# The last MLP-2 group of a hybrid trunk layer: another order of tiles, and another split of the finishing work between engines

## The chip, the cores and the metric

The kernel runs on one core of a Trainium2 chip. The metric is the device time of one execution in microseconds (us). All times below are us from the start of the profiled execution's span unless they say otherwise. TensorE (PE) multiplies, VectorE (DVE) and ScalarE (ACT) work element by element, POOL is GpSimd, and SP issues DMAs in the order in which the program gives them.

## The reference, cut to what matters

One trunk layer is computed for 1024 latent tokens and 128 context tokens. Only its last part bears on the change: the second product of the MLP, its RMS norm, and the gated sum.

```python
f = jnp.square(jax.nn.relu(jnp.einsum('btd,df->btf', h, lp['w_mlp1'])))
f = jnp.einsum('btf,fd->btd', f, lp['w_mlp2'])
x = x + gate2 * rms_norm(f, lp['g_post_mlp'])
```

`gate2` is one row of 1024 for latent tokens and another for context tokens, and the width of f is 4096. The outputs that the change touches are `y_sample` (tiles 0 to 7 of 128 tokens) and `y_prompt` (tile 8).

## The kernel before, in words

The nine token tiles keep an accumulator each in SBUF, `acc_t[i]`, 128 tokens x 1024. The 4096 rows of the second weight are worked off in eight groups (`mlp2(g, hooks)`, L2378, called from L2530). In a group, tile 8 comes first: two halves of 512 columns, 12 products each, into banks `s` and `P` (L2380 to L2389). Then come four rounds u over the pairs of tiles in `QUAD` (L2247), (0, 3), (1, 4), (2, 5), (6, 7), each of seven steps s by a Strassen-like scheme (`STEP2`, L2248): a step (u, s) has six products of 128x512, three on each half `e` of the round's activations. The text calls them round u and step (u, s). Steps of one round that share a letter in `STEP2` (x, y, z) accumulate in the same PSUM bank, and after every step `take` (L2340, L2344) has VectorE add the bank to an accumulator: x is steps 0, 2, 4, 6, z is steps 3 and 5. TensorE can go on in a bank only when it has been taken. Step 5 of a round completes its second tile, step 6 its first.

The activations of a round, `fT`, are two loads of 0.92 MB each (L2326) into one of two sets of buffers. `group_hooks` (L2414) puts the loads of round u + 2 behind step (u, 6) of round u, since they need its buffers: rounds 2 and 3 of a group are loaded behind (0, 6) and (1, 6), rounds 0 and 1 of the next behind (2, 6) and (3, 6). Every DMA here is issued by SP, in program order, and SP waits for whatever the next one needs.

In the last group, functions in `hooks` and two tables place the rest of the work by step. `Gate` (L1721) prepares the gate rows in `fz`: two GRd loads of 0.52 MB, and per quarter of 256 columns a bias row and a norm row (0.13 MB each, L1733, L1734), which VectorE adds and multiplies (`make`, L1740, L1741). Two quarters are made at (0, 4) and (0, 5), which then load the other two into the same two buffers (`mw`), made at (1, 2) and (1, 3). `x1_load(n)` (L2353) loads the residual of tile `FIN[n]`, 0.52 MB, into one of seven buffers `xs`: n = 0 to 6 at the steps (0, 0) to (0, 6), the last two when `finish_b` has freed a buffer. `finish_a(i)` (L2346) has ScalarE square the tile with a sum (L2348) and take the root (L2349); `finish_b(i)` (L2357) has VectorE take the reciprocal (L2359) and do a scaled multiply with the gate in two halves (L2364), and POOL add the residual (L2366; VectorE for the last tile), then SP stores the tile. `FIN` (L2351) is the order of finishing, `FA` and `FH` (L2411, L2412) the steps behind which each half stands. Tiles 7 and 6 are finished after the last step.

Every engine runs its own instructions in order: a gate operation that waits on VectorE holds the takes behind it.

## Time and profile before

| what | us |
|---|---|
| median of 3 runs | 1718.33 |
| lowest and highest of them | 1717.26, 1722.8 |
| the profiled execution's own time | 1720.11 |
| its span | 1718.3 |
| last group, first product | 1656.48 |
| last product of the kernel | ends at 1706.14 |
| busy in the span: PE, DVE, ACT, POOL | 1591.1, 1107.6, 803.4, 518.5 |

The span is the time between the first and the last recorded event of one execution; 1.8 us of that execution's time lie around it. A row of the timeline gives start, length, engine (PEld is TensorE's weight load, SPq is SP's DMA queue), line, operation, output and inputs by the program's names, shape and count; in brackets stands how long the engine was idle before and what released it. Consecutive instructions of one kind are merged into one row. The ends of products are modelled.

### The profile page before, as it was taken

The page shows a single profiled execution, that of the slowest core. Times are in us where ns is not written, and L with a number is a line of the kernel's source. Part 1 is how long each engine was busy: PE and PEld are TensorE (multiplying, and loading weights), DVE is VectorE, ACT ScalarE, POOL GpSimd, SP SyncE. Part 2 cuts the span into 40 slices and gives each one's busy share as a digit, 9 for nine tenths or more (in the row PEclk, how much of TensorE's full clock was granted, in tenths as well). Part 3 has the DMA queues.
Part 4 walks back from the last instruction along what each step waited for, and adds up shares of the span by engine and source line. Part 5 has one row for each costly group of instructions (what it writes and reads, how often), then busy time and mean ns, then how long its engine had stood idle before and what let it go on. Part 6 is the DMA issues. An engine that isn't in the chain of part 4 may idle for free.

```text
span 1718.3 us, 33433 instructions
## 1 busy us (share of the span) xinstructions
PE 1591.1 (93%) x13035; PEld 1341.4 (78%) x13035; DVE 1107.6 (64%) x1884; ACT 803.4 (47%) x1549; POOL 518.5 (30%) x593
## 2 busy tenths in 40 slices
PE   6799989889899999779998999999998899999996
PEld 2678777778788776657686999999998678888884
DVE  2734776586876887947648976777767334444457
ACT  3634443343425567626345666666676422222111
POOL 3100186767310220112120000000000487666635
PEclk9899989999999999989999999999999999999999
DMA  9544856674753768899843568777778755566667
GB/s 312 190 135 125 208 139 173 167 197 116 184 140 93 173 138 196 194 232 246 233 172 112 153 196 243 224 229 221 217 226 276 259 199 215 220 231 233 231 241 256
DMA packets 436030, 341.22 MB, mean 199 GB/s; under 512 B 106392, under 2 KB 396384, under 8 KB 435872
## 3 DMA queue, kind: packets, MB, share of 16 engines
q1 hardware_dynamic: 433760, 331.53, 66.0%
q0 software_dynamic: 2112, 7.55, 1.4%
q8 instruction: 102, 1.67, 0.4%
q14 instruction: 56, 0.46, 0.1%
HBM read 214.72 MB, written 124.29 MB: 197 GB/s over the span
## 4 chain that ended last, share of the span: by engine, by line
PE 68%; DVE 13%; DMA 7%; POOL 4%; ACT 4%; issue 3%; SPq 1%; DVEq 0%; POOLq 0%; ACTq 0%
PE ps_g L2399 9%; PE ps_g L2222 6%; PE ps_P L2222 6%; PE ps_G L2399 4%; PE ps_g L531 4%; PE ps_g L532 3%; PE ps_g L533 3%; PE ps_G L2222 3%; PE ps_g L1662 3%; PE ps_m L2399 2%; PE ps_m L1534 2%; PE ps_G L1503 2%; PE ps_m L2222 2%; DMA wm<-in_w_mod_dram 2%; PE ps_G L1519 2%
## 5 line engine op out<-in xcount | busy, mean ns | idle before, releaser
L531 PE MATMUL ps_g<-hH,wH 128*128 128x384 f32 x552 | 208.3, 377 | 2.6 <-DVE hH L270 1.9
L532 PE MATMUL ps_g<-hL,wH 128*128 128x384 f32 x552 | 190.8, 346 | 6.5 <-DVE hL L484 6.1
L533 PE MATMUL ps_g<-hH,wL 128*128 128x384 f32 x552 | 189.2, 343 | 0.0
L2312 POOL TENSOR_TENSOR sL<-w2r,sL 128x512 fp32r<-128x512 f32 x8 | 10.4, 1302 | 451.6 <-ACT sL L2311 451.6
L2344 DVE TENSOR_TENSOR acc<-ps_g,acc 128x512 f32<-128x512 f32 x116 | 80.0, 691 | 94.0 <-PE ps_g L2399 80.1
L531 PEld LDWEIGHTS ps_g<-hH,wH 128*128 128x128 f32 x552 | 107.0, 194 | 18.0 <-issue 8.4
L2222 PE MATMUL ps_P<-h2H,ws 128*128 128x384 f32 x432 | 118.3, 334 | 0.0
L532 PEld LDWEIGHTS ps_g<-hL,wH 128*128 128x128 f32 x552 | 107.3, 194 | 11.2 <-DVE hL L484 10.0
L2399 PE MATMUL ps_g<-sH,fT 128*128 128x512 f32 x408 | 109.9, 401 | 1.1 <-DVE acc L2344 1.1
L533 PEld LDWEIGHTS ps_g<-hH,wL 128*128 128x128 f32 x552 | 106.8, 194 | 0.0
L2399 PEld LDWEIGHTS ps_g<-sH,fT 128*128 128x128 f32 x408 | 77.7, 191 | 21.0 <-DVE acc L2344 2.4
L1024 POOL TENSOR_TENSOR ar<-ar 128x252 f32<-128x252 f32 (+22 forms) x124 | 80.8, 652 | 42.2 <-DMA ar<-NAd 33.4
L2120 ACT ACTIVATE ft<-ft 128x384 f32<-128x384 f32 x138 | 72.3, 524 | 42.4 <-DVE ft L2119 39.4
L1028 POOL TENSOR_TENSOR ar<-ar 128x252 f32<-128x252 f32 (+22 forms) x124 | 86.5, 697 | 9.2
L2222 PEld LDWEIGHTS ps_P<-h2H,ws 128*128 128x128 f32 x432 | 78.7, 188 | 0.0
L2399 PE MATMUL ps_G<-sL,fT 128*128 128x512 f32 x252 | 70.3, 401 | 5.2 <-ACT acc L2342 5.0
L2222 PE MATMUL ps_P<-h2L,ws 128*128 128x384 f32 x216 | 72.2, 334 | 0.0
L1539 DVE TENSOR_TENSOR SV<-ps_m,Dt 64x256 f32<-64x256 f32 x136 | 57.1, 421 | 23.3 <-PE ps_m L1534 17.0
L2344 DVE TENSOR_TENSOR acc<-ps_G,acc 128x512 f32<-128x512 f32 x60 | 41.4, 690 | 38.4 <-PE ps_G L2399 38.4
L2222 PE MATMUL ps_G<-oT,ws 128*128 128x384 f32 x336 | 63.9, 338 | 0.2 <-DVE ft L2119 0.2
L2311 ACT ACTIVATE sL<-tt 128x512 fp32r<-128x512 f32 x31 | 19.6, 632 | 94.1 <-POOL tt L2305 62.6
L2222 PE MATMUL ps_g<-oT,ws 128*128 128x384 f32 x336 | 63.0, 336 | 0.0
(522 smaller groups left out, 4177.0 us busy)
## 6 DMA issues: line engine op xcount, KB each, us to landing
Fd<-fs SPq DMA_DIRECT2D x224, 256.0 KB
fT<-Fd SPq DMA_DIRECT2D x64, 896.0 KB
KGd<-ar SPq DMA_DIRECT2D x96, 192.0 KB
r<-KGd SPq DMA_DIRECT2D x36, 512.0 KB
mw<-in_w_mod_dram SPq DMA_DIRECT2D x64, 256.0 KB
w1r<-in_w_mlp_dram SPq DMA_DIRECT2D x32, 512.0 KB
w2r<-in_w_mlp_dram SPq DMA_DIRECT2D x31, 512.0 KB
raw<-in_w_in_dram SPq DMA_DIRECT2D x26, 512.0 KB
```

The lines of the kernel that those rows point to most:

```text
L531: T.matmul(ps, wH[:, k, :], hH[b][:, k, :], start=(k == 0), stop=False)
L532: T.matmul(ps, wH[:, k, :], hL[b][:, k, :], start=False, stop=False)
L533: T.matmul(ps, wL[:, k, :], hH[b][:, k, :], start=False, stop=(k == 7))
L1024: E.tensor_tensor(out=t, in0=X[:, :, 0:m, j:j + 1].to_broadcast([128, 2, m, w]), in1=n[:, :, j % 8:j % 8 + 1, j + 1:32].to_broadcast([128, ...
L1028: E.tensor_tensor(out=X[:, :, 0:m, j + 1:32], in0=X[:, :, 0:m, j + 1:32], in1=t, op=ALU.subtract)
L1503: T.matmul(RU[n][r0:r0 + 32, 0, p, :], KRG[n][kq][:, e, p, kc, 0:32], SV[n][s % NSV][:, e, p, :], start=True, stop=True)
L1539: Q.add("V", cv(256), lambda e=e, ks=ks: V.tensor_tensor(out=SV[n][(s + 1) % NSV][ks, e], in0=x["S"][ks], in1=dv[ks], op=ALU.mult), r=[("S ...
L1662: T.matmul(z["ps"], y["t"][:, q // 2, k], wo_t[4 + k][q % 2][:, hs_], start=first, stop=last and stop)
L2120: S_ = lambda: [S.activation(out=f, in_=x, func=fn) for x, fn in ((src if add is None else f, AF.Relu), (f, AF.Square))]
L2222: T.matmul(ps[ch], w[:, qw, k], h[q][:, k, :], start=(new and k == n == 0), stop=(k == 3 and n == 2), skip_group_check=True)
L2344: V.tensor_tensor(out=acc_(i, h), in0=ps, in1=acc_(i, h), op=ALU.add)
L2399: T.matmul(ps[ch], f[:, OPI[fx], qf], w[:, qw], start=(new and e == n == 0), stop=(e == 1 and n == 2), skip_group_check=True)
```

## The change

In the last group, tile 8 comes after the four rounds (`unit_c`), and `FIN` puts it last. All four quarters of the gate's rows are loaded ahead of the first step, into two buffers (`r2`, `r3`) that the weights have left, and the eight gate operations stand one per step from (0, 2) to (1, 2). The residual loads 0 to 4 stand at (0, 1) to (0, 5), loads 5 and 6, into `r2` and `r3`, at (1, 5) and (1, 6). Tiles 3 and 0 (`FINP`) are finished at (1, 2): ScalarE scales them by the reciprocal, POOL multiplies with the gate and adds the residual, in halves. The other seven tiles are finished by VectorE alone, as four operations (multiply, add, multiply, add) that go into a list `dq`; from step (2, 4) on `pop` lets one out behind every step, three ahead of each take of tile 8, and the rest at the end. `finish_a` works on tile 8 in halves, as each is complete. Results are written into the accumulator rather than into the residual's buffer, and every output is stored in halves of 0.26 MB.

```diff
--- before.py
+++ after.py
@@ -1733,12 +1733,13 @@
             SY.dma_start(out=t[:, 0], in_=a["b_mod"][0, j * D + 256 * h:j * D + 256 * h + 256].partition_broadcast(128))
             SY.dma_start(out=t[:, 1], in_=a[self.gp][0, hs_].partition_broadcast(128))
 
-        def make(self, h):
+        def make(self, h, q=None):
             hs_ = slice(256 * h, 256 * h + 256)
             bb, gb = [self.t[h][:, q:q + 1].to_broadcast([128, 2, 256]) for q in range(2)]
             r = self.rows[:, :, hs_]
-            V.tensor_tensor(out=r, in0=r, in1=bb, op=ALU.add)
-            V.tensor_tensor(out=r, in0=r, in1=gb, op=ALU.mult)
+            for n, (x, op) in enumerate(((bb, ALU.add), (gb, ALU.mult))):
+                if q in (None, n):
+                    V.tensor_tensor(out=r, in0=r, in1=x, op=op)
 
     def gtmp(h):
         return wp.tile([128, 4, 128], F32, tag="mw", name="mw", bufs=2).rearrange("q (a b) d -> q a (b d)", a=2)
@@ -2343,40 +2344,65 @@
         else:
             V.tensor_tensor(out=acc_(i, h), in0=ps, in1=acc_(i, h), op=ALU.add)
 
-    def finish_a(i):
-        ss = fin_ss[i] = mp["ac"].tile([128, 1], F32, tag="ss", name="ss", bufs=4)
-        S.activation(out=wp.tile([128, D], F32, tag="raw", name="jk", bufs=1), in_=acc_t[i], func=AF.Square, accum_out=ss)
-        S.activation(out=ss, in_=ss, func=AF.Sqrt, scale=1.0 / D, bias=eps[:, 0:1])
-
-    FIN = (8, 3, 0, 4, 1, 5, 2, 7, 6)
+    FIN = (3, 0, 4, 1, 5, 2, 7, 6, 8)
+
+    FINP = (3, 0)
+    dq = []
+
+    def finish_a(i, h=None):
+
+        c = slice(0, D) if h is None else slice(512 * h, 512 * h + 512)
+        ss = mp["ac"].tile([128, 1], F32, tag="ss", name="ss", bufs=6)
+        S.activation(out=wp.tile([128, D], F32, tag="raw", name="jk", bufs=1)[:, c], in_=acc_t[i][:, c], func=AF.Square, accum_out=ss)
+        if h == 1:
+            V.tensor_tensor(out=ss, in0=ss, in1=fin_ss[i], op=ALU.add)
+        fin_ss[i] = ss
+        if h != 0:
+            S.activation(out=ss, in_=ss, func=AF.Sqrt, scale=1.0 / D, bias=eps[:, 0:1])
+            finish_b(i)
 
     def x1_load(n):
         x1_t[FIN[n]] = xs[n % 7]
         SY.dma_start(out=xs[n % 7], in_=X1d[FIN[n]][:])
 
     def finish_b(i):
-        ss, xt, t = fin_ss[i], x1_t[i], acc_t[i]
-        V.reciprocal(out=ss, in_=ss)
+        ss, t = fin_ss[i], acc_t[i]
+        gt, m = gt2["t"][:, 0 if i < 8 else 1], FIN.index(i)
         dst = o["sample"][0, 128 * i:128 * i + 128] if i < 8 else o["prompt"][0]
-        end = FIN.index(i) > 6
+        if i in FINP:
+            V.reciprocal(out=ss, in_=ss)
+            S.activation(out=t, in_=t, func=AF.Copy, scale=ss)
         for h in range(2):
             hs_ = slice(512 * h, 512 * h + 512)
-            V.scalar_tensor_tensor(out=t[:, hs_], in0=t[:, hs_], scalar=ss, in1=gt2["t"][:, 0 if i < 8 else 1, hs_], op0=ALU.mult,
-                                   op1=ALU.mult)
-            (V if i == FIN[-1] else G).tensor_tensor(out=xt[:, hs_], in0=t[:, hs_], in1=xt[:, hs_], op=ALU.add)
-            if end:
-                SY.dma_start(out=dst[:, hs_], in_=xt[:, hs_])
-        if not end:
-            SY.dma_start(out=dst, in_=xt)
-        if FIN.index(i) + 7 < NTILE:
-            x1_load(FIN.index(i) + 7)
+            if i in FINP:
+                G.tensor_tensor(out=t[:, hs_], in0=t[:, hs_], in1=gt[:, hs_], op=ALU.mult)
+                G.tensor_tensor(out=t[:, hs_], in0=t[:, hs_], in1=x1_t[i][:, hs_], op=ALU.add)
+                SY.dma_start(out=dst[:, hs_], in_=t[:, hs_])
+                if h and m + 7 < NTILE:
+                    x1_load(m + 7)
+                continue
+
+            def op1(h=h, hs_=hs_):
+                if h == 0:
+                    V.reciprocal(out=ss, in_=ss)
+                V.scalar_tensor_tensor(out=t[:, hs_], in0=t[:, hs_], scalar=ss, in1=gt[:, hs_], op0=ALU.mult, op1=ALU.mult)
+
+            def op2(h=h, hs_=hs_):
+                V.tensor_tensor(out=t[:, hs_], in0=t[:, hs_], in1=x1_t[i][:, hs_], op=ALU.add)
+                SY.dma_start(out=dst[:, hs_], in_=t[:, hs_])
+                if h and m + 7 < NTILE:
+                    x1_load(m + 7)
+            dq.extend((op1, op2))
+
+    def pop(n=1):
+        for q in range(min(n, len(dq))):
+            dq.pop(0)()
 
     def run(hooks, k):
         for fn in hooks.get(k, ()):
             fn()
 
-    def mlp2(g, hooks):
-        last = g == NG2 - 1
+    def unit_c(g, hooks):
         for h in range(2):
             ps = bank("sP"[h])
             for e in range(2):
@@ -2385,8 +2411,19 @@
                     w = w2[g, e, f"B{m + 1}{h + 1}"]
                     for n, (qf, qw) in enumerate(TERMS):
                         T.matmul(ps, f[:, 7 + m, qf], w[:, qw], start=(e == m == n == 0), stop=(e == m == 1 and n == 2))
+            if g == NG2 - 1:
+                pop(3)
             take(g, 8, h, ps, True)
+            if g == NG2 - 1:
+                finish_a(8, h)
             run(hooks, ("c", h))
+
+    FA = {(1, 2): (3, 0), (1, 5): (4,), (1, 6): (1,), (2, 5): (5,), (2, 6): (2,), (3, 5): (7,), (3, 6): (6,)}
+
+    def mlp2(g, hooks):
+        last = g == NG2 - 1
+        if not last:
+            unit_c(g, hooks)
         for u, (i, j) in enumerate(QUAD):
             ps = {}
             for s_, (fx, wx, ch) in enumerate(STEP2):
@@ -2400,16 +2437,14 @@
                                  skip_group_check=True)
                 take(g, *((i, 0), (i, 0), (j, 0), (j, 1), (j, 1), (j, 0), (i, 1))[s_], ps[ch], s_ in (0, 2, 3, 6))
                 run(hooks, (u, s_))
-                if last and (u, s_) in FH:
-                    finish_b(FH[u, s_])
-                if last and (u, s_) in FA:
-                    finish_a(FA[u, s_])
+                if last:
+                    for q in FA.get((u, s_), ()):
+                        finish_a(q)
+                    if (u, s_) >= (2, 4):
+                        pop()
         if last:
-            finish_a(6)
-            finish_b(7)
-            finish_b(6)
-    FH = {(1, 4): 8, (1, 6): 3, (2, 1): 0, (2, 3): 4, (2, 6): 1, (3, 2): 5, (3, 4): 2}
-    FA = {(0, 6): 8, (1, 2): 3, (1, 5): 0, (2, 0): 4, (2, 2): 1, (3, 0): 5, (3, 1): 2, (3, 5): 7}
+            unit_c(g, hooks)
+            pop(99)
 
     def group_hooks(g):
 
@@ -2515,18 +2550,21 @@
         if g == NG2 - 1:
             fz = [act.tile([128, 3072], F32, tag=f"h{q}1", name=f"fz{q}") for q in "HL"]
             gt2["t"] = fz[0][:, 0:2048].rearrange("p (m d) -> p m d", m=2)
+            gq = [mp["ac"].tile([128, 2, 2, 256], F32, tag=t, name="gq") for t in ("r2", "r3")]
             xs.extend([fz[0][:, 2048:3072]] + [fz[1][:, 1024 * q:1024 * q + 1024] for q in range(3)] +
-                      [mp["ac"].tile([128, D], F32, tag=t, name="xq") for t in ("q0", "r2", "r3")])
-            g2 = Gate(gt2["t"], 1, "g_post_mlp", gtmp)
-            for h in range(2):
+                      [mp["ac"].tile([128, D], F32, tag="q0", name="xq")])
+            g2 = Gate(gt2["t"], 1, "g_post_mlp", lambda h: gq[h // 2][:, h % 2])
+            hk = lambda u, s_, fn: hooks.setdefault((u, s_), []).append(fn)
+            for h in range(4):
                 g2.load(h)
-            hk = lambda u, s_, fn: hooks.setdefault((u, s_), []).append(fn)
-            for h in range(2):
-                hk(0, 4 + h, lambda h=h: g2.make(h))
-                hk(0, 4 + h, lambda h=h: g2.load(h + 2))
-                hk(1, 2 + h, lambda h=h: g2.make(h + 2))
-            for n in range(7):
-                hk(0, n, lambda n=n: x1_load(n))
+                for q in range(2):
+                    n = 2 + 2 * h + q
+                    hk(n // 7, n % 7, lambda h=h, q=q: g2.make(h, q))
+            for n in range(5):
+                hk(0, 1 + n, lambda n=n: x1_load(n))
+            for n in (5, 6):
+                hk(1, n, lambda n=n: xs.append(mp["ac"].tile([128, D], F32, tag=f"r{n - 3}", name="xq")))
+                hk(1, n, lambda n=n: x1_load(n))
         mlp2(g, hooks)
     pD.close()
     pP.close()
```

## Rows read from the trace of the kernel before

**Rows 1.** The page of the profile, its first line.

```profile
span 1718.3 us, 33433 instructions
```

**Rows 2.** Windows: stretch, us, busy (count) of PE, PEld, DVE, ACT, POOL; PEclk, DMA, GB/s.

```profile
1662.20:1706.20 44.00, 41.18 (x169) 30.56 (x167) 35.82 (x57) 10.01 (x21) 18.65 (x13) 1.00 0.87 302
```

**Rows 3.** Chain of waits that ended last: start, length, what.

```profile
1663.61 1.39 PE ps_m L2399 x6
...
1675.25 9.46 DMA fT<-Fd
...
1688.25 8.13 DMA fT<-Fd
...
1713.90 0.69 DVE fzL L2366
```

**Rows 4.** Timeline: start, length, engine, line, operation, count; last takes and product.

```profile
1656.68 0.69 DVE L2344 TENSOR_TENSOR acc<-ps_g,acc 128x512 f32<-128x512 f32 x1 [0.71 <-PE ps_g L2399]
...
1662.25 0.69 DVE L2344 TENSOR_TENSOR acc<-ps_P,acc 128x512 f32<-128x512 f32 x1 [2.09 <-PE ps_P L2387]
...
1704.58 1.56 PE L2399 MATMUL ps_g<-sH,fT 128*128 128x512 f32 x6
```

**Rows 5.** Timeline of SP's queue at the start of the last group.

```profile
1657.04 0.99 SPq L1732 DMA_DIRECT2D fzH<-GRd  x2
```

**Rows 6.** SP's waits, 1655 to 1672; one x1 load in a narrow stretch.

```profile
SPq L2355 <- DMA fzH<-GRd: 2.5, 2, 1.5
...
L2355 SPq DMA_DIRECT2D fzL<-X1d x1: 320/320/320, 1665.8 to 1665.8; - x1
```

**Rows 7.** Timeline of VectorE: the first gate operations and a take.

```profile
1669.85 0.68 DVE L1740 TENSOR_TENSOR fzH<-fzH,mw 128x512 f32<-128x512 f32 x1
1670.57 0.69 DVE L1741 TENSOR_TENSOR fzH<-fzH,mw 128x512 f32<-128x512 f32 x1
1671.18 0.68 DVE L2344 TENSOR_TENSOR acc<-ps_G,acc 128x512 f32<-128x512 f32 x1
```

**Rows 8.** Windows (columns as in rows 2), two pauses of TensorE: granted clock.

```profile
216.50:223.50 7.00, 6.83 (x27) 6.33 (x26) 1.90 (x3) 4.93 (x9) 6.17 (x10) 0.52 0.89 218
441.80:445.50 3.70, 0.00 (x0) 0.00 (x0) 1.43 (x2) 0.81 (x3) 1.90 (x8) 0.95 0.43 116
445.50:448.50 3.00, 2.98 (x12) 2.89 (x13) 2.20 (x5) 2.40 (x6) 0.08 (x3) 0.50 0.88 212
```

**Rows 9.** Timeline of ScalarE: square and root of one tile.

```profile
1682.92 1.06 ACT L2348 ACTIVATE jk<-acc 128x1024 f32<-128x1024 f32 x1 [7.62 <-DVE acc L2344]
...
1684.11 0.29 ACT L2349 ACTIVATE ss<-ss,eps 128x1 f32<-128x1 f32 x1
```

**Rows 10.** Windows (columns as in rows 2): DMA share and GB/s of two stretches.

```profile
1657.50:1671.50 14.00, 14.00 (x62) 11.31 (x61) 6.37 (x10) 2.08 (x4) 1.33 (x2) 1.00 1.00 378
1672.00:1685.00 13.00, 11.44 (x47) 8.11 (x46) 11.68 (x19) 4.83 (x10) 2.94 (x2) 1.00 0.88 300
```

**Rows 11.** POOL's groups in the last group: busy, mean ns, idle before.

```profile
L2366 POOL TENSOR_TENSOR fzL<-acc,fzL 128x512 f32<-128x512 f32 x6 | 9.0, 1516 | 1.9 <-DVE acc L2364 1.9
...
L2312 POOL TENSOR_TENSOR s<-tt,s 128x512 fp32r<-128x512 f32 x1 | 1.3, 1294 | 0.7 <-ACT s L2311 0.7
```

**Rows 12.** Timeline of SP's queue: the load of round 3.

```profile
1687.36 0.32 SPq L2355 DMA_DIRECT2D fzH<-X1d  x1
1687.77 0.86 SPq L2326 DMA_DIRECT2D fT<-Fd  x2
```

**Rows 13.** VectorE: timeline of a reciprocal, a late multiply; all eighteen multiplies.

```profile
1680.68 0.15 DVE L2359 RECIPROCAL ss<-ss 128x1 f32<-128x1 f32 x1
1680.87 1.42 DVE L2364 SCALAR_TENSOR_TENSOR acc<-acc,ss,fzH 128x512 f32<-128x512 f32 x2
...
1713.05 0.74 DVE L2364 SCALAR_TENSOR_TENSOR acc<-acc,ss,fzH 128x512 f32<-128x512 f32 x1
...
L2364 DVE SCALAR_TENSOR_TENSOR acc<-acc,ss,fzH x18: 737/750/1656, 1680.9 to 1713.1; 128x512 f32<-128x512 f32 x18
```

## The prediction

> **What bounds the kernel now.** I read the page first (span 1718.3 [rows 1]), then the stretch that the change edits: the last of eight MLP-2 groups, from 1656.5 us. Its windows and the chain that ended last come next, then the single instructions of each engine and of SP's queue.
>
> TensorE carries the group. A step of six products takes 1.40, tile 8's two banks 5.57 (1656.68 to 1662.25), and the last product ends at 1706.14 [rows 2 to 4]. In the 44.0 us of the 28 quad steps TensorE is busy 41.2, and some of that is stretched work: 28 x 1.40 is 39.2, so 4.9 is lost, to takes that VectorE does late and to transposed-activation loads (`fT`) that land late: the chain holds two of these, 9.46 and 8.13 long [rows 2, 3]. From 1706.14 to the end, 12.2 us, VectorE and POOL finish tiles. The last VectorE operation ends at 1714.59 [rows 3], 3.7 ahead of the span's end. The question is whether the change shortens what comes before the last product by more than it lengthens what follows.
>
> Without any wait, step (u, s) of the changed order begins at 1656.5 + 1.40 x (7u + s), since tile 8 no longer stands ahead of it: the quads could end at 1695.7.
>
> **Gate rows, on the path.** The gate's eight VectorE operations start at step (0,2), not (0,4), and the group itself begins 5.57 earlier. The first needs both GRd rows, issued from 1657.04 behind the `fT` load, and the first bias row, issued behind those [rows 5]. An x1 load that waited for GRd was issued at 1665.8 [rows 6]: so that is when GRd is there. The same transfers stand ahead of it after the change. The bias row is next, 0.13 MB, so I take 1666.1. VectorE reaches the operation at 1661.5 and stands still, and behind it in its queue stands take(0,3). The operation and the take start 0.61 apart [rows 7], so the take ends at 1667.4. TensorE may not begin step (0,5), which adds to the same bank, before: wanted at 1663.5, it begins 3.9 late. Bounds: 3.4, if GRd alone decides; 7.6, if the bias row lands only by 1669.85, where VectorE now reads it without a wait [rows 7]. I take 3.9, nearest to the load seen waiting.
>
> Such a pause costs clock as well. After 3.7 us of idle at 441.8 to 445.5 the granted clock was 0.50, the lower level (1.2 GHz), for the next 3.0 us: 1.5 lost; elsewhere it stood near it for 7 us: 3.5 lost [rows 8]. I take 1.5, the row whose pause is like this one; bounds 0 and 3.5. Step (1,2)'s take so starts at 1656.7 + 14.0 + 3.9 + 1.5 = 1676.1.
>
> **Tiles 3 and 0, hidden work that reaches SP's queue.** Both are finished at (1,2), in program order: ScalarE squares, VectorE's reciprocal, ScalarE's scaling, four POOL operations, two outputs and an x1 load on SP; then the same for tile 0. VectorE's take and last gate operation put the first reciprocal at 1677.4, the scaling (as long as the square, 1.06 [rows 9]) ends at 1678.7. Only then can ScalarE square tile 0, since it runs in order: square to root took 1.48 [rows 9], so VectorE stands before tile 0's reciprocal until 1680.2 and take(1,3) ends at 1681.1. Step (1,5) was due at 1678.7: 2.4 late. Round 2 then begins at 1683.9 and ends at 1693.7. Its own load is no bound: 8.4 MB up to and with it (two `fT` of 1.84, GRd 1.05, gate rows 1.05, five x1 2.62) at the 378 GB/s seen from 1657.5 [rows 10] is there at 1679.7.
>
> POOL starts at 1678.8: eight operations of 1.30, the 128x512 row without a neighbour on VectorE, are 10.4 (12 by the 1.5 of those that had one [rows 11]): done at 1689.2. Here is the price. SP issues in order: the last output of tile 0 waits for POOL, and behind it stand x1 loads 8 and 5 and, from step (1,6), the `fT` load of round 3. It is issued about 1690.5, though its buffer was free by 1683.9.
>
> **When round 3's load lands.** Before, the load issued at 1687.77, with one x1 load 0.4 ahead of it, landed 8.13 after 1688.25 [rows 3, 12]: 9.0 us after that first issue for 2.36 MB, while an output issued behind it moved along. Now it is 3.14 MB (an output 0.26, two x1, the load) from 1689.2. The extra 0.78 MB costs 2.1 to 2.6 at the 378 or the 300 GB/s of two stretches [rows 10]; I take 2.2, near the one in which the engines were never idle: second half at 1700.4, first half (0.92 MB) 2.4 sooner. Less would be taken if what is issued behind a load cost it nothing: 0.52 MB at 378, 1.4 to 1.5, second half at 1698.9. The Trainium skill ("DMA: Bandwidth & Descriptors", Queues, rings and completion order) says that each DMA engine takes descriptors in the order of its ring, so that the x1 load issued behind costs nothing; by it the landing would be 1698.9 and the end 1.5 sooner. The rows speak for the slower case: 3.90 MB had moved from 1672 to 1685.0 [rows 10], which is everything issued there, the x1 load behind the `fT` load included, and that `fT` load landed at 1684.71 [rows 3].
>
> Round 3, ready at 1693.7, so waits until 1698.0 for the first three products and 1700.4 for the next: it ends at 1700.4 + 0.7 + 6 x 1.40 = 1709.5, and with 1.5 of clock again [rows 8] at 1711.0. The 2.4 of the step before are inside this wait and cost nothing more.
>
> **The tail.** VectorE takes over what POOL added for tiles 4, 1, 5, 2, 7: 28 operations wait in a list, one is let out per step from (2,4): 10 by (3,6), of which the tenth comes after the last quad take. 19 then stand after that take: 9 multiplies and 10 adds. A multiply and the add that needs it start 0.85 apart (1713.05, 1713.90), an add and the next operation 0.61 [rows 3, 7, 13]: 9 x 0.85 + 10 x 0.61 = 13.8. Four reciprocals add 0.19 each [rows 13]: 0.8; three takes 1.8; VectorE's wait for the square of tile 8's second half (half of 1.06, a readout, a small add) 1.2. Sum 17.6. With 3.7 for the last output: 21.3 from the end of the quads to the end of the span, against 12.2 before. Tile 8's 5.57 of products lie wholly beside it. Bounds: 19.8 (no gap between multiply and add, half the wait) to 22.5. Moving adds off POOL does spare VectorE the multiplies that took up to 1656 ns against 737 [rows 13], but those it had beside TensorE's work.
>
> **Sum.** 1695.7 + 3.9 + 1.5 + 2.4 + 6.0 (round 3's wait for its load: its end at 1709.5, not 1703.5) + 1.5 + 21.3 = 1732.3, against 1718.3: 14.0 more. The profiled execution took 1720.11, 1.8 above the median of the runs, 1718.33; so I put the 14.0 onto that median: **1732.3**. Removed at no cost: 5.57 of products ahead of the quads, whose cover (late `fT` loads) comes back in round 3. Steps (2,4) to (3,6) hold a take and one operation, 0.61 + 0.72 to 0.85 against 1.40, so VectorE keeps up there without holding TensorE.
>
> **Rivals.**
> *Round 3's load is on time, the gate rows are not.* It would need SP to pass POOL's outputs sooner, or POOL to start sooner. Round 3 then ends at 1703.5: 1724.8. Against it: before, outputs that wait for POOL already held this load until 1687.77 [rows 12]. Chance 0.14.
> *No change: the transfers land when they are asked for.* The place is SP's stream from 1656 on: GRd and the first bias row there by 1662, round 3's load by 1689. Then only the 2.4 on ScalarE's order is left, the quads end at 1698.1 and the span at 1719.4. It decides as long as the waits together stay below 4.1. For it: the new order has no gate-row loads waiting on VectorE in SP's queue. Against: [rows 6]. Chance 0.14.
> *Slower still.* Both pauses cost 3.5 of clock [rows 8] and POOL runs at 1.5: 1737.7. Chance 0.06.
> *Faster.* Even without any wait 1695.7 + 19.8 = 1715.5, not yet faster by what can be told; it takes an error in my count of VectorE's work after the quads. Chance 0.04.
> *The forecast*, 1724 to 1737: chance 0.62.
>
> **Numbers.** A measurement tells some 0.3% (5.2) from no change: below 1713.2 faster, above 1723.5 slower. Slower holds the forecast, the first and the third rival nearly whole: 0.80; within 0.3% the second and a little of the first: 0.16; faster 0.04. The range 1720 to 1738 leaves out the faster case, half of the second rival and most of the third.
>
> **What would show it.** In the changed trace: VectorE idle before the first gate operation until about 1666, its releaser a GRd or bias transfer; TensorE's step (0,5) near 1667 and a granted clock of 0.5 soon after; SP's `fT` load for round 3 issued near 1690, close behind an output that waited for POOL; TensorE waiting for `fT` at round 3's start; VectorE without a gap after the last quad step, some 17 us to its last add. I am wrong if the gate operation finds its rows at 1661.5, if round 3's load is issued before 1686, or if VectorE's work after the quads is under 14 us.

## The result, and the profile after

The changed kernel takes 1735.9 us in the median of four runs (1732.8 to 1737.34), the kernel before 1717.8 in its four: the ratio is 1.0095, with an interval of 1.0073 to 1.0116. The change makes it slower: by 18.1 between the two medians, by 16.3 (12.5 to 19.9) going by the ratio, where 14.0 was forecast. Timed again later, beside other runs of the kernel before, the ratio was 1.0070 [1.0047, 1.0093], that is 12.0.

The work ahead of the last group is the same in all kernels here, but for 1.05 MB of rows that three of them load in the group before; that group takes 44.8 in the kernel before and in these. Yet the last group began anywhere from 1647.8 to 1658.3 in the profiled executions. So traces are compared by the **length of the last group**, from its first product to the end of the span: 61.8 before (1656.48 to 1718.3), 74.6 after (1656.38 to 1731.0), 12.8 more.

The page's first line and its busy times, against [rows 1]:

```profile
span 1731.0 us, 33454 instructions
...
PE 1589.1 (92%) x13035; PEld 1340.1 (77%) x13035; DVE 1108.8 (64%) x1893; ACT 805.6 (47%) x1553; POOL 502.2 (29%) x585
```

No engine has more than 2.2 us more to do (before, PE was at 1591.1, DVE at 1107.6, ACT at 803.4). What was added is waiting. The timeline of the last group after the change; these rows answer to [rows 4 to 7, 9, 11 to 13] (POOL's and SP's stand together, out of the order of time):

```profile
1657.09 0.86 PE L2436 MATMUL ps_g<-s,fT 128*128 128x512 f32 x3
1657.79 0.86 PE L2436 MATMUL ps_m<-sL,fT 128*128 128x512 f32 x3
...
1666.27 0.69 DVE L1742 TENSOR_TENSOR fzH<-fzH,gq 128x512 f32<-128x512 f32 x1 [4.80 <-DMA gq<-in_b_mod_dram]
1666.88 0.68 DVE L2345 TENSOR_TENSOR acc<-ps_G,acc 128x512 f32<-128x512 f32 x1
1667.62 1.65 PE L2436 MATMUL ps_G<-sL,fT 128*128 128x512 f32 x3 [4.08 <-DVE acc L2345]
...
1677.45 0.16 DVE L2373 RECIPROCAL ss<-ss 128x1 f32<-128x1 f32 x1
1680.19 0.16 DVE L2373 RECIPROCAL ss<-ss 128x1 f32<-128x1 f32 x1 [2.59 <-ACT ss L2361]
1681.00 0.96 PE L2436 MATMUL ps_G<-sL,fT 128*128 128x512 f32 x3 [2.00 <-DVE acc L2345]
...
1678.88 1.26 POOL L2378 TENSOR_TENSOR acc<-acc,fzH 128x512 f32<-128x512 f32 x1 [19.39 <-ACT acc L2374]
...
1688.06 1.30 POOL L2379 TENSOR_TENSOR acc<-acc,fzL 128x512 f32<-128x512 f32 x1
...
1686.76 2.96 SPq L2380 DMA_DIRECT2D out_dram<-acc  x2
1689.77 0.42 SPq L2366 DMA_DIRECT2D fzL<-X1d  x1
1690.28 0.40 SPq L2366 DMA_DIRECT2D xq<-X1d  x1
1690.77 0.86 SPq L2327 DMA_DIRECT2D fT<-Fd  x2
...
1697.34 1.20 PE L2436 MATMUL ps_g<-sL,fT 128*128 128x512 f32 x3 [3.50 <-DMA fT<-Fd]
1699.72 1.65 PE L2436 MATMUL ps_g<-s,fT 128*128 128x512 f32 x3 [1.18 <-DMA fT<-Fd]
...
1711.44 0.69 DVE L2345 TENSOR_TENSOR acc<-ps_g,acc 128x512 f32<-128x512 f32 x1
...
1719.02 0.16 DVE L2358 TENSOR_TENSOR ss<-ss 128x1 f32<-128x1 f32 x1 [0.85 <-ACT jk L2356]
...
1726.63 0.74 DVE L2388 SCALAR_TENSOR_TENSOR acc<-acc,ss,fzH 128x512 f32<-128x512 f32 x1
1727.41 0.69 DVE L2391 TENSOR_TENSOR acc<-acc,fzL 128x512 f32<-128x512 f32 x1
```

Read it by the brackets, which give the idle time ahead of a row and what ended it. VectorE stands 4.80 before the first gate operation, for a bias row; the take behind it is late, and TensorE stands 4.08 before step (0,5). At (1,2) VectorE stands 2.59 for ScalarE, TensorE 2.00. POOL's eight operations run from 1678.88 to 1689.36; SP's two outputs of tile 0 need them, and only behind these and two x1 loads comes round 3's `fT` load, at 1690.77. TensorE waits for its halves, 3.50 and 1.18. From the last quad take (1711.44) to the span's end 19.56 us pass; the text calls this the tail. The chain of waits names the two transfers, against the two `fT` loads of [rows 3]:

```profile
1658.13 7.95 DMA gq<-in_b_mod_dram
1691.25 8.43 DMA fT<-Fd
```

The windows after, with the columns of [rows 2]: the quads, then the stretches behind the three pauses (two rows for the last). The third number from the end of a row is the granted clock; 0.50 is half speed.

```profile
1656.40:1711.44 55.04, 44.29 (x171) 34.15 (x170) 30.21 (x50) 12.05 (x22) 12.51 (x10) 0.91 0.70 262
1667.60:1670.50 2.90, 2.88 (x7) 2.30 (x8) 1.76 (x3) 0.00 (x0) 0.00 (x0) 0.50 0.93 275
1681.00:1684.00 3.00, 3.00 (x13) 2.46 (x14) 1.38 (x2) 1.12 (x2) 2.92 (x3) 1.00 0.24 95
1697.30:1701.00 3.70, 2.48 (x6) 1.57 (x7) 0.00 (x0) 0.00 (x0) 0.00 (x0) 0.58 0.96 367
1701.00:1705.00 4.00, 4.00 (x11) 3.09 (x11) 2.29 (x5) 0.00 (x0) 0.00 (x0) 0.54 0.17 68
```

The **ledger** adds the length up from its parts. It uses 39.4 for quads without a wait, which a run below shows. Before: 39.4, tile 8's 5.6 ahead of them, 5.0 lost, and 11.8 from the last take to the end make 61.8. After: the quads take 55.0, 15.6 more than 39.4. Of these, 10.8 are waits (4.08 + 2.00 + 3.50 + 1.18) and 4.1 the lower clock: the twelve products from 1667.62 to 1671.87 took 1.45 more than their 2.8, and the eighteen from 1697.34 to 1705.58, less 1.34 for the second wait for the load, 2.7 more than 4.2. The last 0.7 are nearly all a matter of counting. Three products last 0.86 by their modelled end, but the next three start 0.70 behind them (the first two rows above); so each of the four waits, counted from start to start, is 0.16 longer than its bracket, 0.6 in all. With the tail of 19.6: 74.6. So 10.6 went away (5.6 + 5.0), and 15.6 + 7.8 came.

### The profile page after: what moved, and what is told of

Read it like the earlier page. It is cut to its first block, busy times and chain, and to the rows that moved or that the text cites. A ratio compares the mean times of both kernels' runs of the same rounds, so it can differ in the third digit from the quotient of the medians.

```text
span 1731.0 us, 33454 instructions
## 1 busy us (share of the span) xinstructions
PE 1589.1 (92%) x13035; PEld 1340.1 (77%) x13035; DVE 1108.8 (64%) x1893; ACT 805.6 (47%) x1553; POOL 502.2 (29%) x585
## 4 chain that ended last, share of the span: by engine, by line
PE 65%; DVE 15%; DMA 7%; POOL 4%; ACT 4%; issue 3%; SPq 1%; DVEq 0%; ACTq 0%; POOLq 0%
PE ps_g L2436 9%; PE ps_g L2223 6%; PE ps_P L2223 6%; PE ps_G L2436 5%; PE ps_g L531 4%; PE ps_g L532 3%; PE ps_g L533 3%; PE ps_G L2223 3%; PE ps_g L1662 3%; PE ps_m L2436 2%; PE ps_G L1503 2%; PE ps_m L1534 2%; PE ps_G L1519 2%; DMA wm<-in_w_mod_dram 2%; PE ps_m L2223 2%
## 5 line engine op out<-in xcount | busy, mean ns | idle before, releaser
L2436 PE MATMUL ps_G<-sL,fT 128*128 128x512 f32 x252 | 70.6, 402 | 10.5 <-DVE acc L2345 6.1
L2345 DVE TENSOR_TENSOR acc<-ps_G,acc 128x512 f32<-128x512 f32 x60 | 41.5, 691 | 40.6 <-PE ps_G L2436 40.4
L2436 PEld LDWEIGHTS ps_G<-sL,fT 128*128 128x128 f32 x252 | 47.8, 191 | 23.5 <-DVE acc L2345 6.9
L1503 PE MATMUL ps_G<-SV,r 128*32 128x64 f32 x1152 | 53.4, 227 | 11.3 <-DVE SV L1539 9.2
```

Of the source, the lines that this page charges most:

```text
L1503: T.matmul(RU[n][r0:r0 + 32, 0, p, :], KRG[n][kq][:, e, p, kc, 0:32], SV[n][s % NSV][:, e, p, :], start=True, stop=True)
L2345: V.tensor_tensor(out=acc_(i, h), in0=ps, in1=acc_(i, h), op=ALU.add)
L2436: T.matmul(ps[ch], f[:, OPI[fx], qf], w[:, qw], start=(new and e == n == 0), stop=(e == 1 and n == 2), skip_group_check=True)
```

## The experiments

The theory: three waits (gate rows; ScalarE's order at (1,2); round 3's load behind POOL's outputs) and a tail of VectorE work make the time. Rivals: VectorE is the bound as a whole, so that mending waits gains little; or the DMA engines are full, so that a transfer sent earlier only makes another late. All kernels below compute the whole result. Where an expectation names a span, it counts from the changed kernel's start of the group; less 1656.4 it is the length to compare, and so it stands in the table. The kernel before was timed beside each set of runs. Each length is that of one profiled execution; two kernels were profiled twice, and theirs repeat within 0.6.

| run | us | ratio to before | last group | expected |
|---|---|---|---|---|
| before | 1717.62 to 1720.45 | 1 | 61.8 | |
| changed | 1735.9 | 1.0095 [1.0073, 1.0116] | 74.6 | 75.8 |
| changed, again | 1732.18 | 1.0070 [1.0047, 1.0093] | 74.0 | |
| gate rows first | 1727.42 | 1.0060 [1.0040, 1.0081] | 71.9 | 69.1 |
| outputs later | 1725.71 | 1.0042 [1.0019, 1.0065] | 70.0 | 66.6 to 68.1 |
| both | 1720.96 | 1.0021 [0.9999, 1.0044] | 66.4 | 60.6 to 62.1 |
| tile 8 first again | 1727.07 | 1.0057 [1.0039, 1.0075] | 72.4 | 71.6 to 72.6 |
| tile 0 two steps later, alone | 1727.84 | 1.0061 [1.0041, 1.0080] | 76.3 | 73.9 to 75.3 |
| both + tile 0 later | 1722.75 | 1.0028 [1.0011, 1.0045] | 64.9 | 62.5 to 63.5 |
| all waits mended | 1714.91 | 0.9974 [0.9952, 0.9995] | 58.1 | 58 to 59.5 |
| the same, tile 8 first | 1716.41 | 0.9980 [0.9962, 0.9998] | 62.5 | 62 to 63 |
| POOL adds | 1709.42 | 0.9954 [0.9936, 0.9972] | 55.0 | 54 to 57 |
| POOL adds, again | 1709.14 | 0.9949 [0.9927, 0.9970] | 55.3 | 55 |

**Gate rows first.** GRd and the first quarter's rows are issued ahead of round 1's load.

```diff
-            if gl < NG2:
+            if gl < NG2 and (gl, ul) != (NG2 - 1, 1):
                 add(u, 6, lambda gl=gl, ul=ul: f_load(gl, ul))
...
                 g2.load(h)
+                if h == 0:
+                    f_load(g, 1)
```

> Only SP's order is edited: the two GRd rows and the first quarter's bias and norm row are issued ahead of round 1's fT load (1.84 MB) and not behind it. Theory of the waits: the first gate operation finds its rows at about 1661.5, TensorE's 4.08 before step (0,5) and some 1.4 of lower clock go, and as POOL's work on tiles 3 and 0 and round 3's load start as much earlier, the whole 5.5 reaches the end: span 1725.5 against 1731.0. Round 3 still waits about 4.7 for its load. Rival 'VectorE is the bound': its list of operations only piles up, the end moves by under 1.5 (1729.5 or later). Rival 'the DMA engines are full': round 1's load, now 1.3 MB later, makes round 1 wait 2 to 4, and 1728 to 1731 come out.

Measured: 71.9, 2.7 shorter, where 5.5 was expected (a span of 1725.5, so 69.1): a miss. The wait did not go, it broke up:

```profile
1660.48 0.69 DVE L1742 TENSOR_TENSOR fzH<-fzH,gq 128x512 f32<-128x512 f32 x1 [1.62 <-DMA gq<-in_b_mod_dram]
...
1666.15 0.69 DVE L1742 TENSOR_TENSOR fzH<-fzH,gq 128x512 f32<-128x512 f32 x1 [3.17 <-DMA gq<-in_b_mod_dram]
...
1669.89 0.96 PE L2436 MATMUL ps_g<-sL,fT 128*128 128x512 f32 x3 [1.75 <-DVE acc L2345]
...
1692.89 1.65 PE L2436 MATMUL ps_g<-sL,fT 128*128 128x512 f32 x3 [3.51 <-DMA fT<-Fd]
```

VectorE waits the same 4.8 in all, now for the first and the second bias row, and TensorE 1.75 at the second; behind that pause nine products took 1.4 more than 2.1, so the clock was not won back either. Round 3's wait stays, 4.2. Of the rival of full DMA engines the sum came (1728 to 1731, so 71.6 to 74.6) but not the place: for round 1's load TensorE waited 0.20 and not 2 to 4. Late were the second quarter's rows, which now stand behind that load in SP's queue.

**Outputs later.** Tile 3's and 0's outputs, with the x1 loads behind them, are issued behind round 3's load.

```diff
-                SY.dma_start(out=dst[:, hs_], in_=t[:, hs_])
+                late_out2.append(lambda hs_=hs_: SY.dma_start(out=dst[:, hs_], in_=t[:, hs_]))
                 if h and m + 7 < NTILE:
-                    x1_load(m + 7)
+                    late_out2.append(lambda: x1_load(m + 7))
...
+                    if (u, s_) == (1, 6):
+                        for fn in late_out2:
+                            fn()
```

> Only SP's order is edited: the four outputs of tiles 3 and 0 and x1 loads 7 and 8, which wait for POOL, are issued behind x1 load 5, round 3's fT load and x1 load 6. Theory of the waits: round 3's load is issued when round 1 leaves its buffer, near 1684 and not at 1690.8, lands by 1691, and round 3 starts without a wait at 1693.7: 4.7 of waiting and some 2 of lower clock go, quads end at 1703.5 to 1704, span 1723 to 1724.5. The gate's wait at 1662 to 1667 stays. Rival 'VectorE is the bound': end at 1729 or later although the wait is gone. Rival 'the DMA engines are full': the load issued at 1684 lands only after 1695, and 1728 or later comes out.

Measured: 70.0, 4.6 shorter; expected were 66.6 to 68.1. Round 3's load is issued at 1685.74 and TensorE doesn't wait for it. That is the causal test of the term: the load was late because it stood behind outputs that wait for POOL. The next wait then shows; timeline and windows of this kernel:

```profile
1682.73 0.96 PE L2436 MATMUL ps_G<-sL,fT 128*128 128x512 f32 x3 [1.99 <-DVE acc L2345]
...
1685.74 1.60 SPq L2327 DMA_DIRECT2D fT<-Fd  x2
```
```profile
1682.70:1684.20 1.50, 1.47 (x6) 1.23 (x7) 0.69 (x1) 0.57 (x1) 1.50 (x2) 1.00 0.03 11
1684.20:1687.20 3.00, 3.00 (x8) 2.33 (x7) 0.87 (x2) 1.45 (x3) 2.84 (x4) 0.50 0.28 38
```

The 1.99 at (1,5) is the changed kernel's 2.00, no longer hidden, and here 3.0 us at the lower clock come 1.5 after it, so 1.5 are lost. Those, and more of the lower clock behind the gate's pause (4.17; fifteen products from 1667.97 to 1674.29 took 2.8 more than 3.5, against 1.45 lost in the changed kernel), are the part that is missing. The edit need not be what lowered the clock: the changed kernel, profiled again below, has the same behind the same pause.

**Both edits.**

```diff
+                if h == 0:
+                    f_load(g, 1)
...
+                late_out2.append(lambda hs_=hs_: SY.dma_start(out=dst[:, hs_], in_=t[:, hs_]))
```

> Both edits of SP's order together. Theory of the waits: the gains add, since the first wait sits ahead of the second: quads end near 1698, span 1717 to 1718.5, within 1.5 of the kernel before. The 2.0 wait on ScalarE's order at step (1,5) and the 19.6 after the quads stay. Rival 'VectorE is the bound': no earlier than 1726. Rival 'the DMA engines are full': round 1 or 3 waits for its load all the same, 1721 to 1727.

Measured: 66.4, that is 8.2 shorter, where the single edits gave 2.7 and 4.6; 60.6 to 62.1 was expected, since I had taken every wait but the one at (1,5) as gone. The sum lies in the range of the DMA rival (1721 to 1727, so 64.6 to 70.6). TensorE still waits 0.84, 0.24 and 1.76 around the gate and 1.99 at (1,5), behind which 1.6 go to the lower clock; round 3 doesn't wait. The tail is the same 19.6, and the length is still 4.6 over the kernel before.

**Tile 8 first again**, all else as changed, but that tile 8's square is one piece again and its takes have no list operations ahead of them.

```diff
-        if not last:
-            unit_c(g, hooks)
+        unit_c(g, hooks)
...
-            unit_c(g, hooks)
+            finish_a(8)
             pop(99)
```

> The changed kernel with the one move undone: tile 8's products stand ahead of the quads again in the last group; tile 8 is still finished last, from one square of the whole row. Theory of the waits: the quads start 5.57 later, so the gate rows are there when VectorE asks, its 4.8 and TensorE's 4.08 and 1.4 of clock vanish, and the quads end where they did, near 1711; behind them 18 operations stand without tile 8's two takes and its wait for the square, so span 1728 to 1729: moving tile 8 last gained nothing, even cost 2. Rival 'the order is a gain and the split between engines the loss': the end is 3 to 5.5 later, 1734 to 1736.

Measured: 72.4, as expected. The move itself costs 2.2 of the 12.8. Tile 8's products cover the gate rows, whose wait is gone; the other two stay:

```profile
1675.06 0.96 PE L2431 MATMUL ps_G<-sL,fT 128*128 128x512 f32 x3 [2.00 <-DVE acc L2345]
...
1691.41 1.16 PE L2431 MATMUL ps_g<-sL,fT 128*128 128x512 f32 x3 [3.52 <-DMA fT<-Fd]
1693.79 1.65 PE L2431 MATMUL ps_g<-s,fT 128*128 128x512 f32 x3 [1.21 <-DMA fT<-Fd]
```

**Tile 0 two steps later, alone.** ScalarE's square of tile 0 no longer stands behind tile 3's scaling with VectorE waiting for both.

```diff
-    FA = {(1, 2): (3, 0), (1, 5): (4,), (1, 6): (1,), (2, 5): (5,), (2, 6): (2,), (3, 5): (7,), (3, 6): (6,)}
+    FA = {(1, 2): (3,), (1, 4): (0,), (1, 5): (4,), (1, 6): (1,), (2, 5): (5,), (2, 6): (2,), (3, 5): (7,), (3, 6): (6,)}
```

> The changed kernel with tile 0 finished at (1,4) and not at (1,2), nothing else. Theory: TensorE's 2.0 before step (1,5) goes, but POOL's first tile starts as before and round 3's load is issued behind its last output, so TensorE waits as much longer for that load: length of the last group 74.6 as in the changed kernel, within 0.7. Rival 'every wait of TensorE counts': 72.6 or less.

Measured: 76.3, which is 1.0 above the range. The mechanism came: the wait at (1,5) is gone, and TensorE waits for round 3's load 6.7 instead of 4.7. The 2.0 reappear there, so that term was hidden, as forecast. The 1.7 on top lie where the clock was low: behind the gate's pause, as long as before (4.12), it was at 0.50 for 5 us, not 2.9 (twelve products in 5.2, so 2.4 lost), and behind round 3's wait for 8 us (eighteen products lost 3.6, not 2.7). The runs' times, 1.0061 against 1.0095 and 1.0070, show no such loss; it may be this one execution's:

```profile
1690.13 1.65 PE L2436 MATMUL ps_g<-sL,fT 128*128 128x512 f32 x3 [6.11 <-DMA fT<-Fd]
...
1692.33 1.65 PE L2436 MATMUL ps_g<-s,fT 128*128 128x512 f32 x3 [0.55 <-DMA fT<-Fd]
```
```profile
1659.00:1662.00 3.00, 2.94 (x7) 2.36 (x8) 1.80 (x4) 0.00 (x0) 0.00 (x0) 0.50 0.88 266
1662.00:1664.00 2.00, 2.00 (x6) 1.52 (x6) 1.29 (x2) 1.16 (x3) 0.00 (x0) 0.50 1.03 408
...
1690.00:1694.00 4.00, 3.32 (x7) 2.22 (x8) 0.00 (x0) 0.00 (x0) 0.00 (x0) 0.50 0.83 336
1694.00:1698.00 4.00, 4.00 (x10) 3.09 (x10) 2.68 (x5) 0.00 (x0) 0.00 (x0) 0.50 0.17 66
```

**Both, and tile 0 later.** The two diffs of "both" and the one above.

```diff
+                    f_load(g, 1)
...
+                late_out2.append(lambda hs_=hs_: SY.dma_start(out=dst[:, hs_], in_=t[:, hs_]))
...
+    FA = {(1, 2): (3,), (1, 4): (0,), (1, 5): (4,), (1, 6): (1,), (2, 5): (5,), (2, 6): (2,), (3, 5): (7,), (3, 6): (6,)}
```

> Both edits of SP's order, and tile 0 is finished at step (1,4) and not with tile 3 at (1,2). Measured as the length of the last group, first product to the end of the span (66.4 with both edits of SP's order, 61.8 in the kernel before). Theory: VectorE no longer stands 2.6 before tile 0's reciprocal, TensorE loses neither the 2.0 before step (1,5) nor the lower clock that followed it there: 62.5 to 63.5. The 19.6 from the last quad take to the end stays. Rival 'VectorE is the bound': 65.5 or more.

Measured: 64.9, a miss by 1.4. The wait at (1,5) is gone, and no lower clock is left in the quads; the gate rows still cost 1.09 and 1.72. With round 1 shorter, round 2's load is late, by 0.65 and 1.26. The window from the group's start to its landing shows the DMA engines nearly full (a share of 0.92):

```profile
1682.12 0.96 PE L2436 MATMUL ps_g<-sL,fT 128*128 128x512 f32 x3 [0.65 <-DMA fT<-Fd]
1684.34 0.96 PE L2436 MATMUL ps_g<-s,fT 128*128 128x512 f32 x3 [1.26 <-DMA fT<-Fd]
```
```profile
1658.30:1684.30 26.00, 21.33 (x88) 15.85 (x86) 15.01 (x25) 8.38 (x15) 7.99 (x7) 1.00 0.92 360
```

These are 9.4 MB (26.0 us by 360 GB/s). Up to and with round 2's load 8.4 are issued, so 1.0 of what is issued behind it moved along. Here the rival of full DMA engines holds. The next kernel takes the bias and norm rows, 1.05 MB, out of this stretch, and round 2 doesn't wait; whether another order of the same bytes would do as much was not tried.

**All waits mended.** The bias and norm rows are loaded in the group before, into buffers that are free there; GRd goes into the half of `fz` that comes free a step sooner, ahead of round 1's load; the two edits above stay; and four waiting list operations run while ScalarE squares tile 8's second half.

```diff
+        if g == NG2 - 2:
...
+                for h in range(4):
+                    g2.load(h)
+            hooks.setdefault((2, 0), []).append(early)
...
+            gt2["t"] = fz[1][:, 0:2048].rearrange("p (m d) -> p m d", m=2)
...
+                SY.dma_start(out=gt2["t"][:, m], in_=GRd[1][m].partition_broadcast(128))
+            f_load(g, 1)
...
         if h == 1:
+            pop(4)
             V.tensor_tensor(out=ss, in0=ss, in1=fin_ss[i], op=ALU.add)
```

> As the run with tile 0 at (1,4), and the gate's rows come without a wait: the bias and norm rows are loaded during the group before into two buffers free since then, the GRd rows go into buffers that are free a step sooner, ahead of round 1's load; and VectorE does what is left of tile 6 while ScalarE squares tile 8's second half (0.85 of waiting). Theory of the waits: no wait of TensorE over 0.5 in the quads, which take 39.2 to 39.8; 18.8 from the last take to the end: length 58 to 59.5, against 61.8 before. Rival 'the DMA engines are full': round 1's load late by 1 to 3, 60 to 62.5. Rival 'the move of tile 8 cannot pay': not under 61.8.

Measured: 58.1, as expected, and 0.9974 of before. In the quads TensorE has no wait, at the full clock: this is the 39.4 of the ledger.

```profile
1650.24:1689.63 39.39, 39.39 (x171) 31.65 (x170) 30.32 (x50) 11.91 (x22) 12.58 (x10) 1.00 0.88 333
```

The tail, 18.7, is the rest, 0.9 less than 19.6, since VectorE's wait for the square is filled. So the rival of VectorE as the bound holds for the tail alone, and that of full DMA engines not for this order (it gave 60 to 62.5).

**The same with tile 8 first** (the diff of "tile 8 first again" on this kernel).

```diff
+        unit_c(g, hooks)
...
+            finish_a(8)
```

> The run with all three waits mended (length of the last group 58.1), with tile 8's products ahead of the quads again. Theory: now that nothing else is late, the 5.57 of products in front count: the quads end 5.5 later, and 17.5 follow the last take, where 18.7 did with tile 8 at the end: length 62 to 63, no better than the 61.8 of the kernel before. Rival 'moving tile 8 last is worth nothing even then, VectorE's list is the bound': 58 to 59.5.

Measured: 62.5, as expected. Without waits, moving tile 8 last is worth 4.4 by the lengths (62.5 against 58.1), where in the changed kernel it cost 2.2. The runs' times are too coarse to show it: 4.4 is 0.0026 of the whole, the two ratios are 0.0006 apart, and their intervals reach 0.002 to either side.

**POOL adds.** The gate rows and the list operations beside the square as in "all waits mended", tile 8 last; but no tile is scaled by ScalarE and finished by POOL. All multiplies are VectorE's, and in the quads, from (1,3) on, POOL makes the adds, two list operations at two of three steps; behind the quads VectorE makes both.

```diff
-    FINP = (3, 0)
-    dq = []
+    FINP = ()
+    dq, AE = [], [G]
...
-                V.tensor_tensor(out=t[:, hs_], in0=t[:, hs_], in1=x1_t[i][:, hs_], op=ALU.add)
+                AE[0].tensor_tensor(out=t[:, hs_], in0=t[:, hs_], in1=x1_t[i][:, hs_], op=ALU.add)
...
-                    if (u, s_) >= (2, 4):
-                        pop()
+                    if (u, s_) >= (1, 3) and (7 * u + s_) % 3 != 0:
+                        pop(2)
         if last:
+            AE[0] = V
```

> As the run before in this call, but no tile is finished by ScalarE and POOL, and within the quads the adds are POOL's again: from (1,3) on, at two of every three steps, VectorE does a multiply and POOL the add; after the quads VectorE does both. It undoes 'the others by VectorE alone' where takes run beside. Theory 1, POOL's add holds only VectorE's operations with two SBUF inputs, not the takes: two halves fit into three steps (0.74 + 1.30 each, 4.1 of 4.2), twelve halves are done by the end of the quads, six are left and not nine and a half, 14.9 from the last quad take to the end: length 54 to 57. Theory 2, held multiplies hold the takes behind them as in the kernel before, TensorE waits 3 to 6 again: 58 to 61.

Measured: 55.0, as expected, ratio 0.9954: it beats both the kernel before and the changed one. The quads take 40.4, 1.0 more than 39.4, and the tail 14.6, 4.1 less than 18.7. Its timeline, and the window of its quads:

```profile
1676.23 0.75 DVE L2389 SCALAR_TENSOR_TENSOR acc<-acc,ss,fzL 128x512 f32<-128x512 f32 x1
...
1677.11 1.29 POOL L2392 TENSOR_TENSOR acc<-acc,fzH 128x512 f32<-128x512 f32 x1 [0.97 <-ACT ss L2362]
...
1677.50 1.47 DVE L2389 SCALAR_TENSOR_TENSOR acc<-acc,ss,fzL 128x512 f32<-128x512 f32 x1
...
1678.88 0.68 DVE L2345 TENSOR_TENSOR acc<-ps_m,acc 128x512 f32<-128x512 f32 x1
...
1679.04 1.30 POOL L2392 TENSOR_TENSOR acc<-acc,fzH 128x512 f32<-128x512 f32 x1 [0.64 <-DVE acc L2389]
1679.61 0.69 DVE L2345 TENSOR_TENSOR acc<-ps_g,acc 128x512 f32<-128x512 f32 x1
```
```profile
1655.70:1696.00 40.30, 40.26 (x172) 31.69 (x171) 35.93 (x54) 10.07 (x21) 16.54 (x13) 1.00 0.89 339
```

A multiply, which reads two SBUF operands, takes 1.47 beside POOL's add (1.22 to 1.47 over seven of them) and 0.75 without it (six of six in the quads); a take beside it, which reads PSUM and one SBUF operand, keeps its 0.69. The Trainium skill ("SBUF — State Buffer", Who interferes with whom) says just this: a VectorE instruction with two SBUF inputs contends with a GpSimd instruction that reads SBUF, and one with at most one SBUF input, outside the 2-port perf modes, does not; the trace agrees with both halves, 1.47 and 0.69. So adds on POOL cost VectorE little where takes run beside them, and TensorE is busy in 40.26 of 40.30.

**Again**, without an edit, this kernel and the changed one.

> The same kernel as the run with POOL's adds within the quads, timed in more rounds: length 55 again, and a ratio to the kernel before of 0.995 to 0.997, its interval clear of 1.

> The changed kernel itself, timed on the chip of these runs: the last group is 12.8 longer than in the kernel before by the two profiles, so a ratio of 1.0074 is expected if the rest of the kernel is the same, 1.006 to 1.009. Rival 'something outside the last group is slower as well': 1.0095 or more, as in the first measurement.

Measured: 1709.14, ratio 0.9949, just under the 0.995 to 0.997 expected, and 1732.18, ratio 1.0070, within 1.006 to 1.009; for something slower outside the last group, which would have given 1.0095 or more, the repeat gives no sign. The lengths, 55.3 and 74.0, repeat within 0.6. The changed kernel's second profile has the same pauses at (0,5) and (1,5), 4.19 and 1.99, but another clock behind the second one:

```profile
1680.71 0.96 PE L2436 MATMUL ps_G<-sL,fT 128*128 128x512 f32 x3 [1.99 <-DVE acc L2345]
```
```profile
1682.00:1685.00 3.00, 3.00 (x8) 2.35 (x8) 0.69 (x1) 1.45 (x3) 2.92 (x3) 0.50 0.33 128
```

Round 2 ended 1.5 later for it, and TensorE waited for round 3's load 3.3 and not 4.7; the load's second half was there 43.6 after the group's start, 43.3 in the first profile. So what delays the steps ahead of that load is hidden by it, here as in the run with tile 0 later.

## Why the prediction was right, point by point

As a length the forecast was 75.8 (1732.3 less 1656.5); measured were 74.6 and 74.0. The waits and the tail came where they were forecast. That the sum is so near is partly luck, since the mis-sized terms below have both signs. The median of the runs, 1735.9, is 3.6 above the forecast; the profiled execution, 1732.8, was the fastest of the four.

*Gate rows.* Right: the first gate operation starts at 1666.27 (bias row forecast for 1666.1), step (0,5) 4.08 late (3.9). The clock behind it cost 1.45 (1.5). This last agreement is luck: behind the same pause it cost 1.65, 2.4 and 2.8 in three other executions.

*Tiles 3 and 0.* Right: reciprocals at 1677.45 and 1680.19 (1677.4, 1680.2); the step at (1,5) waited 2.00 where I counted 2.4 of delay. POOL ran 1678.88 to 1689.36 (1678.8 to 1689.2). That these 2.0 are hidden by round 3's load is shown from both sides: taken away alone, they come back in that wait; with that wait gone, they stand alone.

*Round 3's load.* The mechanism is right, and shown by issuing the outputs later. The term was mis-sized: 6.0 of waiting forecast, 4.7 measured (5.0 from start to start). The halves came 0.7 sooner, at 1697.34 (1698.0) and 1699.72 (1700.4); another 0.3 is the lower clock of the first three products, which lies within the forecast's wait. The prediction's sentence on the Trainium skill ("DMA: Bandwidth & Descriptors", Queues, rings and completion order) would have put the landing at 1698.9; it lies between the two and decides neither. What that section states is the order in which one DMA engine takes its descriptors; that a load issued behind costs nothing was the prediction's inference, and the 1.0 MB that moved ahead of round 2's landing in "both, and tile 0 later" speak against it. The clock behind round 3's wait cost 2.7, not 1.5; the two errors cancel, and the last quad take, at 1711.44, came 0.4 after the forecast's end of the quads.

*The tail.* Mis-sized, and just outside its own bounds of 19.8 to 22.5: 21.3 forecast, 19.6 measured. VectorE's part was 16.7 (1711.44 to 1728.10), not 17.6: multiply and add start 0.78 apart (1726.63, 1727.41), not 0.85, which is 0.6 over nine pairs, and the wait for tile 8's square was 0.85 of the 1.2 that I had for it and its small operations. Then 2.9 to the end of the span, not 3.7. That VectorE bounds this part is shown by its 0.85 of idle time in these 16.7 and by the runs that change its work there: 18.7 with that wait filled, 14.6 with fewer operations left behind the quads, and 19.5 to 19.7 in every run that keeps its order, whatever came ahead.

*The rivals.* Of the rival in which the transfers land when they are asked for nothing came. The rival of round 3 on time is what "outputs later" made by hand: 70.0, 8.2 over before, where 6.5 was worked out: the clock cost 2.8 and about 1.6 behind its two pauses, where I had 1.5 for one, and the tail 1.7 less. The price of the slower rival is 1737.9 by its own terms (2.0 more of clock twice, 1.6 more on POOL) and not 1737.7; nothing rests on it.

Two things stay open: why the clock's price differs between executions, and why the span ends 2.9 to 3.0 after VectorE in the changed kernels and 3.7 in the one before.

## What to carry to other kernels

Work that is moved ahead can meet its operands' landing, and what hurt here was less the operation that waits than the one in order behind it: a take behind a gate operation, and a load behind an output in SP's queue. Before an output is given to an in-order queue, look at what must be issued behind it; a mended wait shows the next one, so compare stage by stage, and judge a reordering again once its waits are mended (tile 8 last: 2.2 worse, then 4.4 better, by the lengths). Work can be shared between VectorE and POOL at little cost while VectorE's own instructions read PSUM and one SBUF operand.

## What the runs showed that was not expected

- The price of a pause in clock isn't fixed, not even in one kernel. After 2.00 of pause at (1,5) the granted clock stayed 1.00 in the changed kernel's first profile; after 1.99 there it was 0.50, the lower level (1.2 GHz), for 3.0 us in its second, and so it was with the outputs later. Up to step (0,5) the changed kernel, "outputs later" and "tile 0 two steps later" are one program: after 4.08 and 4.19 (the changed kernel's two), 4.17 and 4.12 of pause the lower clock cost 1.45, 1.65, 2.8 and 2.4. So the length of a kernel with such pauses can be 1 to 2 us off for this alone; the kernels with all waits mended and with POOL's adds have no pause in the quads.
- The profiled executions of kernels with the same work ahead reached the last group up to 10.5 us apart (1647.8 to 1658.3), and the runs of one kernel spread more (1703.28 to 1720.92 for the best one); so effects of 2 to 5 us were read from lengths of the stage.
